# Row-wise softmax: the late loads on ScalarE's DMA queue, and a second and third tile of 5 and 15 rows

## The chip, the core and the metric

The kernel runs on one core of a Trainium2 chip. The metric is the time of one execution on the device, in microseconds (us). Two times occur below: the time of an execution, and its span in the profile, from the first to the last thing that the profile shows.

## What is computed

A softmax with temperature 2 over the last axis of an array of 16 x 1024 x 512 floats, 33.55 MB in and as much out:

```python
x_scaled = x / 2.0
x_max = np.max(x_scaled, axis=-1, keepdims=True)
exp_x = np.exp(x_scaled - x_max)
return exp_x / np.sum(exp_x, axis=-1, keepdims=True)
```

The kernel first computes exp(x / 2) / sum(exp(x / 2)) without the maximum. At the end it counts the rows whose sum lies between 1 and 1e30; if any does not, a second pass with the maximum is run over everything. With the data of this case the second pass is skipped.

## The kernel before

The 16384 rows are spread over 128 partitions, 128 rows of 512 floats in each. "A row" below is one such row in every partition: 128 x 512 floats, 262,144 bytes. The 128 rows are cut into ten tiles (`TILES`, line 10: rows, and place in the on-chip buffer `arena`). `arena` has 98 rows, too few for all 128, so the last two tiles reuse places: tile 8 lies where tiles 0, 1 and 2 were, tile 9 where the end of tile 2 and the start of tile 3 were. `LATE` (line 14) names whose stores must have landed before each may be loaded. These two are called the late loads.

*Loads.* Tile 0 is loaded from SyncE's DMA queue, tiles 1 to 7 from ScalarE's, all issued at the start (`early`, line 146, and `loads`, line 150). A load is one DMA of 128 pieces, one a partition, each as long as the tile's rows. Tile 1 (`SPREAD`) is loaded in three DMAs: all rows but the last over 128 partitions, then the last row over 126 and over 2 partitions (line 111).

*Exponentials.* ScalarE takes the rows in order, in chunks (`HEAD`, then chunks of `E` = 5). For each chunk it waits for `s_go`, which TensorE's queue raises when a tile's load has landed (line 185). It computes the exponential of each row in place, with the row's sum (lines 195 and 269). The chunks of `HEAD`, 23 rows, are straight code; the other 105 rows run in a loop (`exponentials`, line 257).

*Division.* VectorE takes the chunks of a tile in pairs: one reciprocal of the sums (line 160), one multiply in place (line 163). A tile of 15 rows is a pair of 10 rows and a single of 5.

*Stores.* SyncE issues them in order of tiles. `store` (line 127) waits until VectorE is done with the tile. `s_home` counts the landings of stores 0 to 3, on which the late loads depend; `s_end` counts the others, and SyncE waits for it last (line 255). The two late loads stand in SyncE's program among the stores:

```python
for t in (0, 1, 2, 3):
    store(nc.sync, t)
for t, then in ((8, (4,)), (9, (5, 6, 7, 8, 9))):
    nc.sync.wait_ge(s_home[t], landings(LATE[t]))
    load(nc.sync, t)
    for u in then:
        store(nc.sync, u)
```

An engine's program runs in order, so a wait in it holds all that stands behind it. DMAs issued from one engine go into one queue (q1 is SyncE's, q10 ScalarE's in the profile); both queues are served by the same 16 DMA engines. After the exponentials ScalarE's program has only the read of the flag that decides on the second pass.

Of the kernel before, what the change touches and what calls it, by code (L numbers as in the profile page):

```python
# [7 lines left out]


TILES = [  # L10
    (3, 0), (7, 3), (13, 10), (15, 23), (15, 38), (15, 53), (15, 68), (15, 83), (15, 0), (15, 15),
]

LATE = {8: (0, 1, 2), 9: (3,)}
ARENA = 98

HEAD = [3, 4, 3, 5, 4, 4]
E = 5

SPREAD = 1  # L20

LO, HI = 1.0, 1.0e30
G = 8
# [3 lines left out]
def kernel(  # L27
# [5 lines left out]
    nc = tc.nc  # L33
# [10 lines left out]
    n_rows = N // P  # L44
# [13 lines left out]
    tiles, base = [], 0  # L58
# [5 lines left out]
    def dram(ap, t):  # L64
        b, r, _ = tiles[t]
        return ap[b * P : (b + r) * P].rearrange("(p r) d -> p r d", r=r)

    def sb(t):
        _, r, at = tiles[t]
        return arena[:, at : at + r, :]  # L70

    straight = sum(HEAD)
    sizes = HEAD + [E] * ((n_rows - straight) // E)
    starts = [sum(sizes[:k]) for k in range(len(sizes))]
# [14 lines left out]
    s_home = {t: nc.alloc_semaphore(f"s_home{t}") for t in LATE}  # L89
# [17 lines left out]
    def load(eng, t):  # L107
        r = tiles[t][1]
        parts = [(0, P, 0, r)]
        if t == SPREAD:  # L110
            parts = [(0, P, 0, r - 1), (0, 126, r - 1, r), (126, P, r - 1, r)]
        for p, q, lo, hi in parts:
            eng.dma_start(
                out=sb(t)[p:q, lo:hi], in_=dram(xf, t)[p:q, lo:hi]
            ).then_inc(ld[t], 16)
# [6 lines left out]
    def landings(ts):  # L122
        return 16 * len(list(ts))
# [3 lines left out]
    def store(eng, t):  # L127
        eng.wait_ge(s_mul, upto[t])
        eng.dma_start(out=dram(of, t), in_=sb(t)).then_inc(stored_by.get(t, s_end), 16)

    def take(eng, sem, n):
        eng.wait_ge(sem, n).then_inc(sem, -n)  # L132

    def rounds(eng, body, step=1):

        last = n_rows // G
        i = eng.alloc_register("tile")
        eng.wait_ge(s_flag, 1)  # L140
        eng.reg_load(i, flag[0:1, 0:1])
        with eng.While(lambda: eng.snap(i, min_val=0, max_val=last) < last):
            body(eng.snap(i, min_val=0, max_val=last - 1))
            eng.reg_add(i, i, step)
# [9 lines left out]
    def program():  # L154

        nc.vector.memset(ones[:, :], 1.0).then_inc(s_ones, 1)  # L156
        for j, ks in enumerate(pairs):
            b, c = starts[ks[0]], sum(sizes[k] for k in ks)
            a = b % ARENA
            nc.vector.reciprocal(  # L160
                out=recip[:, b : b + c], in_=stats[:, b : b + c]
            )._wait_ge(s_exp, ks[-1] + 1).then_inc(s_rec, 1)
            nc.vector.tensor_mul(  # L163
                out=arena[:, a : a + c],
                in0=arena[:, a : a + c],
                in1=recip[:, b : b + c].unsqueeze(2).to_broadcast([P, c, D]),
            )._wait_ge(s_rec, j + 1).then_inc(s_mul, 1)
        nc.vector.tensor_scalar(  # L168
            out=inside[:, :], in0=stats[:, :], scalar1=LO, scalar2=HI,
            op0=Alu.max, op1=Alu.min,  # L170
        ).then_inc(s_cnt, 1)
        nc.vector.tensor_tensor(  # L172
            out=inside[:, :], in0=inside[:, :], in1=stats[:, :], op=Alu.is_equal
        )._wait_ge(s_cnt, 1).then_inc(s_cnt, 1)
        nc.vector.reduce_sum(  # L175
            out=count[:, :], in_=inside[:, :], axis=mybir.AxisListType.X
        )._wait_ge(s_cnt, 2).then_inc(s_cnt, 1)
        nc.vector.tensor_scalar(  # L178
            out=flag[:, :], in0=total[:, :], scalar1=float(N), scalar2=float(n_rows // G),
            op0=Alu.is_ge, op1=Alu.mult,  # L180
        )._wait_ge(s_tot, 1).then_inc(s_flag, 1)


        for t in range(len(tiles)):
            nc.tensor.wait_ge(ld[t], 48 if t == SPREAD else 16).then_inc(s_go, owner.count(t))
        nc.tensor.wait_ge(s_ones, 1)
        nc.tensor.matmul(  # L187
            total[:, :], lhsT=count[:, :], rhs=ones[:, :], start=True, stop=True
        )._wait_ge(s_cnt, 3).then_inc(s_tot, 1)

        nc.scalar.preload_act_table(Exp)  # L191
        for k, c in enumerate(HEAD):
            take(nc.scalar, s_go, 1)
            for b in range(starts[k], starts[k] + c):
                ins = nc.scalar.activation(  # L195
                    out=arena[:, b], in_=arena[:, b], func=Exp, scale=0.5,
                    accum_out=stats[:, b : b + 1],
                )
            ins.then_inc(s_exp, 1)
        exponentials(straight, n_rows)  # L200

        for t in (0, 1, 2, 3):
            store(nc.sync, t)
        for t, then in ((8, (4,)), (9, (5, 6, 7, 8, 9))):
            nc.sync.wait_ge(s_home[t], landings(LATE[t]))
            load(nc.sync, t)
            for u in then:
                store(nc.sync, u)  # L210

        x_g = xf.rearrange("(t p r) d -> t p r d", p=P, r=G)
        o_g = of.rearrange("(t p r) d -> t p r d", p=P, r=G)
        data = arena[:, 0:G]

        def vector(i):
            take(nc.vector, g_go, 1)
            nc.vector.reduce_max(  # L220
                out=g_max[:, :], in_=data, axis=mybir.AxisListType.X, negate=True
            ).then_inc(g_rec, 1)
            take(nc.vector, g_rec, 1)
            nc.vector.tensor_scalar_mul(
                out=g_max[:, :], in0=g_max[:, :], scalar1=0.5
            ).then_inc(g_neg, 1)
            take(nc.vector, g_exp, 1)
            nc.vector.reciprocal(out=g_sum[:, :], in_=g_sum[:, :]).then_inc(g_rec, 1)
            take(nc.vector, g_rec, 1)
            nc.vector.tensor_mul(  # L230
                out=data, in0=data, in1=g_sum[:, :].unsqueeze(2).to_broadcast([P, G, D])
            ).then_inc(g_mul, 1)

        def scalar(i):
            take(nc.scalar, g_neg, 1)
            for r in range(G):
                ins = nc.scalar.activation(
                    out=arena[:, r], in_=arena[:, r], func=Exp, scale=0.5,
                    bias=g_max[:, r : r + 1], accum_out=g_sum[:, r : r + 1],
                )  # L240
            ins.then_inc(g_exp, 1)

        def gpsimd(_):
            nc.gpsimd.wait_ge(s_end, at_end)
            for i in range(n_rows // G):
                nc.gpsimd.dma_start(out=data, in_=x_g[i]).then_inc(g_ld, 16)
                nc.gpsimd.wait_ge(g_ld, 16 * (i + 1)).then_inc(g_go, 1)
                take(nc.gpsimd, g_mul, 1)
                nc.gpsimd.dma_start(out=o_g[i], in_=data).then_inc(g_st, 16)
                nc.gpsimd.wait_ge(g_st, 16 * (i + 1))  # L250

        rounds(nc.vector, vector)
        rounds(nc.scalar, scalar)
        rounds(nc.gpsimd, gpsimd, n_rows // G)
        nc.sync.wait_ge(s_end, at_end)

    def exponentials(first, end):
        row = nc.scalar.alloc_register(f"row{first}")
        nc.scalar.reg_mov(row, first)
        with nc.scalar.While(lambda: nc.scalar.snap(row, min_val=first, max_val=end) < end):  # L260
            now = nc.scalar.snap(row, min_val=first, max_val=end - E)
            take(nc.scalar, s_go, 1)
            at = nc.s_assert_within(
                now % ARENA, 0, ARENA - E,
                skip_runtime_bounds_check_because="no chunk reaches over the arena's end",
            )
            for r in range(E):
                data = arena[:, r : ARENA - E + 1 + r][:, bass.ds(at, 1)]
                ins = nc.scalar.activation(  # L269
                    out=data, in_=data, func=Exp, scale=0.5,  # L270
                    accum_out=stats[:, r : n_rows - E + 1 + r][:, bass.ds(now, 1)],
                )
            ins.then_inc(s_exp, 1)
            nc.scalar.reg_add(row, row, E)
# [12 lines left out]
    nc.switch_body(here, parent=None, valid_engines=[i.engine for i in jumps])  # L287
    loads()
    program()


# [28 lines left out]
```

## Time and profile before

| what | value |
|---|---|
| time, median of 9 runs | 160.46 us (160.21 to 160.72) |
| the profiled execution | 160.48 us |
| its span | 159.1 us |
| busy: VectorE, ScalarE | 74.9 us, 80.5 us |
| one exponential of a row, L269 | 614 ns, 105 times |
| one multiply of 10 rows, of 5 rows, L163 | 5492 ns, 2824 ns |
| late loads issued by SyncE | at 57.30 and 75.57 us |
| last exponential, last multiply end | 125.1 us, 130.9 us |
| last store, from issue to landing | 28.1 us |

In the profile an instruction is named by its engine and line: DVE is VectorE, ACT is ScalarE, PE is TensorE; SPq and ACTq are the programs of SyncE and ScalarE where they issue DMAs or handle semaphores. "Idle before" an instruction is how long its engine stood still, followed by what ended that. The duration of a DMA issue is that of issuing it; where the data lands is told by "us to landing". A DMA share of 1.00 is all 16 DMA engines busy; in a short window it can pass 1, since a packet is counted where it starts.

### The profile page before, as it was taken

Reading aid. Unit: us, or ns where it says so; the run is one execution under the profiler, and the core shown is the slowest. Engines: PE = TensorE matmul, PEld = TensorE weight load, DVE = VectorE, ACT = ScalarE, POOL = GpSimd, SP = SyncE. Lnnn points to the kernel's source line nnn. Section 1 sums busy time; section 2 is a strip of 40 time slices with the busy share of each in tenths; the row PEclk is TensorE's granted clock in tenths of the full one; section 3 lists DMA queues with packets and bytes.
Section 4 is the critical chain, followed back from the end, with each engine's and each line's share of the span. In section 5 each row is a group of like instructions: output and inputs, shape, how many; then the busy total and the mean of one; then the engine's idle time right before and its main releaser. Section 6 shows DMA issues by size and latency. Waiting matters only on the chain. (4 is left out here: it accounts for less than half of the span.)

```text
span 159.1 us, 624 instructions
## 1 busy us (share of the span) xinstructions
PE 0.2 (0%) x2; PEld 0.1 (0%) x2; DVE 74.9 (47%) x41; ACT 80.5 (51%) x257; POOL 0.2 (0%) x4
## 2 busy tenths in 40 slices
PE   0000000000000000000000000000000000000000
PEld 0000000000000000000000000000000000000000
DVE  0044509809923980099104970089898991000000
ACT  0585595598099306970099204999999400000000
POOL 0000000000000000000000000000000000000000
DMA  7999999999999999999999999999999999999995
GB/s 267 444 377 445 446 421 364 424 452 407 448 446 448 421 440 433 433 433 433 433 433 440 425 440 425 440 425 448 409 433 425 440 425 448 427 440 425 448 417 255
DMA packets 3026, 67.13 MB, mean 422 GB/s; under 512 B 336, under 2 KB 336, under 8 KB 720
## 3 DMA queue, kind: packets, MB, share of 16 engines
q1 hardware_dynamic: 1872, 42.21, 62.0%
q10 hardware_dynamic: 1152, 24.90, 37.0%
q14 instruction: 2, 0.02, 0.0%
HBM read 33.55 MB, written 33.55 MB: 422 GB/s over the span
## 5 line engine op out<-in xcount | busy, mean ns | idle before, releaser
L269 ACT ACTIVATE arena<-arena x105 | 64.3, 614 | 34.5 <-ACTq L132 25.6
L163 DVE TENSOR_TENSOR arena<-arena,recip 128x5120 f32<-128x5120 f32 (+5 forms) x18 | 71.1, 3951 | 0.6
L160 DVE RECIPROCAL recip<-stats 128x10 f32<-128x10 f32 (+5 forms) x18 | 3.5, 197 | 53.5 <-ACT arena L269 38.9
L269 ACT ACTIVATION_READ_ACCUMULATOR arena<-arena x105 | 19.6, 186 | 0.0
L195 ACT ACTIVATE arena<-arena 128x512 f32<-128x512 f32 x23 | 14.1, 615 | 4.3 <-ACTq L132 4.2
L191 ACT ACT_TABLE_LOAD x1 | 1.3, 1283 | 5.9 <-issue 5.9
L195 ACT ACTIVATION_READ_ACCUMULATOR arena<-arena 128x1 f32 x23 | 4.3, 186 | 0.0
L156 DVE MEMSET ones<- 128x1 f32 x1 | 0.1, 59 | 2.7 <-PEq L35 2.7
L187 PE MATMUL total<-ones,count 128*1 128x1 f32 x2 | 0.2, 164 | 131.8 <-DVE count L175 131.8
L172 DVE TENSOR_TENSOR inside<-inside,stats 128x128 f32<-128x128 f32 x1 | 0.3, 293 | 0.0
L175 DVE TENSOR_REDUCE count<-inside 128x1 f32<-128x128 f32 x1 | 0.3, 286 | 0.0
L178 DVE TENSOR_SCALAR flag<-total 1x1 int32<-1x1 f32 x1 | 0.1, 148 | 0.3 <-PE total L187 0.3
L168 DVE TENSOR_SCALAR inside<-stats 128x128 f32<-128x128 f32 x1 | 0.2, 220 | 0.0
L187 PEld LDWEIGHTS total<-ones,count 128*1 128x1 f32 x2 | 0.1, 80 | 131.8 <-DVE count L175 131.8
L304 POOL MEMSET const-bfloat16-1.0<- 128x1 bf16 x1 | 0.1, 102 | 0.0
L304 POOL MEMSET const-uint8-127<- 128x1 uint8 x1 | 0.1, 101 | 0.0
L304 POOL MEMSET const-float32-0.0<- 128x1 f32 x1 | 0.1, 98 | 0.2 <-issue 0.2
L304 POOL MEMSET const-float32-1.0<- 128x1 f32 x1 | 0.1, 98 | 0.0
## 6 DMA issues: line engine op xcount, KB each, us to landing
out_dram<-arena SPq DMA_DIRECT2D x7, 3840.0 KB, 30.8
arena<-in_x_dram ACTq DMA_DIRECT2D x5, 3840.0 KB, 56.9
arena<-in_x_dram SPq DMA_DIRECT2D x2, 3840.0 KB, 37.2
arena<-in_x_dram ACTq DMA_DIRECT2D x1, 3328.0 KB, 15.0
out_dram<-arena SPq DMA_DIRECT2D x1, 3328.0 KB, 26.2
out_dram<-arena SPq DMA_DIRECT2D x1, 1792.0 KB, 22.0
arena<-in_x_dram ACTq DMA_DIRECT2D x1, 1536.0 KB
arena<-in_x_dram SPq DMA_DIRECT2D x1, 768.0 KB, 6.3
```

Of the source, the lines that this page charges most:

```text
L156: nc.vector.memset(ones[:, :], 1.0).then_inc(s_ones, 1)
L160: nc.vector.reciprocal(out=recip[:, b : b + c], in_=stats[:, b : b + c])._wait_ge(s_exp, ks[-1] + 1).then_inc(s_rec, 1)
L163: nc.vector.tensor_mul(out=arena[:, a : a + c], in0=arena[:, a : a + c], in1=recip[:, b : b + c].unsqueeze(2).to_broadcast([P, c, D]),)._w ...
L168: nc.vector.tensor_scalar(out=inside[:, :], in0=stats[:, :], scalar1=LO, scalar2=HI, op0=Alu.max, op1=Alu.min,).then_inc(s_cnt, 1)
L172: nc.vector.tensor_tensor(out=inside[:, :], in0=inside[:, :], in1=stats[:, :], op=Alu.is_equal)._wait_ge(s_cnt, 1).then_inc(s_cnt, 1)
L175: nc.vector.reduce_sum(out=count[:, :], in_=inside[:, :], axis=mybir.AxisListType.X)._wait_ge(s_cnt, 2).then_inc(s_cnt, 1)
L178: nc.vector.tensor_scalar(out=flag[:, :], in0=total[:, :], scalar1=float(N), scalar2=float(n_rows // G), op0=Alu.is_ge, op1=Alu.mult,)._wa ...
L187: nc.tensor.matmul(total[:, :], lhsT=count[:, :], rhs=ones[:, :], start=True, stop=True)._wait_ge(s_cnt, 3).then_inc(s_tot, 1)
L191: nc.scalar.preload_act_table(Exp)
L195: ins = nc.scalar.activation(out=arena[:, b], in_=arena[:, b], func=Exp, scale=0.5, accum_out=stats[:, b : b + 1],)
L269: ins = nc.scalar.activation(out=data, in_=data, func=Exp, scale=0.5, accum_out=stats[:, r : n_rows - E + 1 + r][:, bass.ds(now, 1)],)
L304: nc = _bacc.Bacc("TRN2", target_bir_lowering=False, num_devices=1)
```

## The change

The second and third tile hold 5 and 15 rows instead of 7 and 13. All tiles but the first are now whole chunks of 5 rows, so `HEAD` is one chunk of 3 rows, and the rest runs in two loops of `exponentials`: up to row 83, the end of tile 6, and from there on. Between the two loops, ScalarE waits for the stores that each late load depends on, and issues both late loads. SyncE issues the stores of tiles 0 to 9 and nothing between them.

```diff
 TILES = [
-    (3, 0), (7, 3), (13, 10), (15, 23), (15, 38), (15, 53), (15, 68), (15, 83), (15, 0), (15, 15),
+    (3, 0), (5, 3), (15, 8), (15, 23), (15, 38), (15, 53), (15, 68), (15, 83), (15, 0), (15, 15),
 ]
 
 LATE = {8: (0, 1, 2), 9: (3,)}
 ARENA = 98
 
-HEAD = [3, 4, 3, 5, 4, 4]
+HEAD = [3]
 E = 5
 
 SPREAD = 1
+
+TURN = 83
...
             ins.then_inc(s_exp, 1)
-        exponentials(straight, n_rows)
-
-
-
-        for t in (0, 1, 2, 3):
+        exponentials(straight, TURN)
+        for t, us in LATE.items():
+            nc.scalar.wait_ge(s_home[t], landings(us))
+            load(nc.scalar, t)
+        exponentials(TURN, n_rows)
+
+        for t in range(len(tiles)):
             store(nc.sync, t)
-        for t, then in ((8, (4,)), (9, (5, 6, 7, 8, 9))):
-            nc.sync.wait_ge(s_home[t], landings(LATE[t]))
-            load(nc.sync, t)
-            for u in then:
-                store(nc.sync, u)
```

## The prediction

> **What bounds the kernel now.** I read the page's slices and queues first, then SyncE's own waits, then the timeline around one tile, then windows of the DMA. The page:
>
> ```profile
> span 159.1 us, 624 instructions
> PE 0.2 (0%) x2; PEld 0.1 (0%) x2; DVE 74.9 (47%) x41; ACT 80.5 (51%) x257; POOL 0.2 (0%) x4
> DMA  7999999999999999999999999999999999999995
> GB/s 267 444 377 445 446 421 364 424 452 407 448 446 448 421 440 433 433 433 433 433 433 440 425 440 425 440 425 448 409 433 425 440 425 448 427 440 425 448 417 255
> HBM read 33.55 MB, written 33.55 MB: 422 GB/s over the span
> ```
>
> The reader is to see that the DMA engines are full in every slice but the first and the last, while no compute engine passes 51%. The bytes are fixed, 67.1 MB; at some 433 GB/s they take 155 us, so all but 4 us of the span is transfer. The change can lose by opening a hole in this row. It can win only out of those 4 us.
>
> Next, SyncE's own waits:
>
> ```profile
> SPq L129 <- DVE arena L163: 96.0, 10, 17.9
> SPq L113 <- DMA out_dram<-arena: 28.5, 2, 16.3
> SPq L255 <- DMA out_dram<-arena: 27.7, 1, 27.7
> ```
>
> The middle row holds the two waits ahead of the late loads (L113), the ones the diff takes from SyncE. The last row is the slack that counts: SyncE has issued the last store and waits 27.7 us for it to land. Writing 3.93 MB at 433 GB/s takes 9.1 us, so for over 17 us that store stands behind older stores. The end of compute is covered by that backlog.
>
> The timeline of one tile (start, us, instruction), its ACT row at the tile's first exponential and its SPq row at the stores from it on:
>
> ```profile
> 61.22 0.63 ACT L269 ACTIVATE arena<-arena  x1 [7.98 <-ACTq L132]
> 79.33 0.63 ACT L269 ACTIVATE arena<-arena  x1 [8.81 <-ACTq L132]
> 97.59 0.63 ACT L269 ACTIVATE arena<-arena  x1 [8.97 <-PEq L185]
> ...
> 94.32 36.96 SPq L129 DMA_DIRECT2D out_dram<-arena  x4
> ...
> 112.58 18.69 SPq L129 DMA_DIRECT2D out_dram<-arena  x3
> ```
>
> ScalarE begins tiles 5, 6 and 7 the moment they land (it idled 8 to 9 us before each), 18.11 and 18.26 us apart. Tile 6 goes from 79.33 to its store at 94.32, tile 7 from 97.59 to 112.58: 14.99 us both times (10 rows of exponentials, a multiply of 5.49, one of 2.82, two reciprocals, handovers). The last SPq row ends with the tenth store, issued about 130.9.
>
> Last, the DMA queues of a stretch with both in use (q10 is ScalarE's, q1 SyncE's), and windows before and after ScalarE's queue runs dry near 96:
>
> ```profile
> DMA packets 529, 14.75 MB, mean 434 GB/s; under 512 B 49, under 2 KB 49, under 8 KB 49
> q1 hardware_dynamic: 272, 7.37, 50.3%
> q10 hardware_dynamic: 257, 7.37, 50.2%
> ...
> 61.00:97.00 36.00, 0.00 (x0) 0.00 (x0) 17.26 (x8) 18.58 (x60) 0.00 (x0) 1.00 1.01 437
> 97.00:131.00 34.00, 0.00 (x0) 0.00 (x0) 25.98 (x13) 27.66 (x90) 0.00 (x0) 1.00 1.00 431
> 131.00:148.00 17.00, 0.19 (x2) 0.09 (x2) 0.78 (x4) 0.00 (x0) 0.00 (x0) 1.00 1.00 432
> ```
>
> From 62 to 96 us the two queues moved 7.37 MB each. So a load that runs beside stores takes twice as long as alone: 18.15 us a tile, the spacing above. One queue alone moves almost as much in total (431 to 432 against 437 GB/s).
>
> **The Trainium skill.** "DMA: Bandwidth & Descriptors", section "Queues, rings and completion order", says each DMA engine takes turns between the queues that have work, packet by packet; the even split agrees. Its section "Issuing engines are not separate DMA queues" says that issuing from several engines only saves the issuer's time; 431 against 437 GB/s agrees to 1.4%. Under "Bandwidth" it puts the ceiling at 435 GB/s; the slices of 433 are at it, so steady state has nothing to give.
>
> **The change part by part.**
>
> *Row split and head.* Tiles 0 to 2 still hold 23 rows. Tile 1's load becomes 4 rows of 2 KB in one piece plus the split row, instead of 6 plus one; tile 2 grows to 15. So 0.52 MB move from 12 KB pieces to 30 KB pieces and 1.05 MB from 12 KB to 8 KB ones. The first 11 us ran at 355 GB/s, startup included. I take 0.1 us of loss, with bounds from -0.3 to +0.3 (1.6 of the 3.9 MB moved there change form, 4.4 us' worth; 7% either way is 0.3). The compute of these tiles changes by a few us: store 1 comes about 3 us earlier (5 rows instead of 7: two exponentials and 1.1 us of multiply less, and the load smaller), store 2 about 2 us later (15 rows, whose path is the 14.99 above). Both lie beside loads queued since 5.9 us, so they cost nothing at the end. VectorE keeps 18 pairs. The rolled loop instead of straight code for 20 rows costs 0.1 to 0.2 us a chunk, on an engine idle 4 us and more before each tile.
>
> *Waits and late loads leave SyncE.* Stores 4 to 9 no longer stand behind loads 8 and 9. Removing 28.5 us of waiting gains nothing directly: both DMA queues had work throughout.
>
> *Waits and late loads come to ScalarE.* They stand after row 83, the end of tile 6: about 79.33 + 9.2 = 88.5 us. By then SyncE's waits on stores 0 to 2 and 3 had already passed (57.30 and 75.57, the late-load issues in its timeline), so I take ScalarE's wait as zero; two issues cost about 1 us (nine took 5.80 at the start), under its 9 us of idle time before tile 7. If a wait did bind, tile 7's exponentials would be behind it; with 8 us to spare from 88.5 to 97.6, I don't expect that.
>
> What decides is when the late loads land. Before, load 8 shared q1 with the stores from 57 us, and load 9 was done at 113.4 (issued 75.57, 37.8 us to landing). After, they queue behind load 7 on q10. By load 7's end both versions have moved equal bytes (store 4 takes load 8's place in q1), so tile 7 still starts at 97.59. Stores 5, 6 and 7 are ready from 76.2, 94.3 and 112.6, so q1 stays filled and the even split goes on:
>
> - tile 8 starts at 97.59 + 18.15 = 115.7, its store is ready at 130.7;
> - tile 9 starts at 97.59 + 36.3 = 133.9;
> - store 9 is issued at 133.9 + 14.99 = 148.9, against 130.9 before: 18 us later.
>
> And when does the backlog run out? Before, store 9 landed at 159.0 (28.1 us after issue). Taking back 9.1 us of data and about 0.5 us of completion (the window 158.00 to 159.10 shows no packet), its data started near 149.4 on the last DMA engine, 148.8 on a typical one. The same bytes precede it after, so the queue empties at 148.8 to 149.4, just when store 9 is issued. A store in an empty queue also pays its first-byte delay, which before hid: the first load, issued at 0.00, shows its first packet at about 1.05 us. So store 9's data runs from 149.9 to 159.0 or 159.2, and landing adds 0.5: 159.6 to 159.8 us. All DMA engines start this store together, which recovers some of their spread.
>
> Sum: first-byte delay bare +1.1, spread recovered -0.4, small pieces +0.1, two-queue stretch longer by 36 us -0.1 (bounds 0 and -0.5, from 437 against 431): about +0.65 us. The profiled execution took 160.48 with a span of 159.05, beside a median of 160.46; so 160.48 + 0.65 = 161.1.
>
> **Rivals.**
>
> *B, covered tail, no change (160.5).* Turns are whole packets: 30 KB at a sixteenth of 433 GB/s, one DMA engine's share, is 1.14 us. If store 0, the first to break into the loads, gets in one packet later relative to tile 2 (now of longer packets), each load is 1.14 us earlier and store 9 is issued at 147.8, in time. For: the moment lies near a packet boundary. Against: the slowest of 16 DMA engines sets a landing, so all must shift.
>
> *C, one turn later (162.2).* The opposite shift: +1.14 us on load 9, all exposed. Against: tile 1's smaller load lets tile 2 start earlier, not later.
>
> *D, faster (159.95).* The two-queue stretch ends near 132 instead of 96; at 437 against 431 GB/s over 36 us it saves 36 x 6/437 = 0.5 us. It decides if load 9 also lands early enough, tile 9 starting by 132.7, for store 9 not to bare its delay. For: the two windows. Against: most of their difference is where packets are counted; single slices in both stretches show 433.
>
> *E, the change doesn't do what it says:* a late store would hold ScalarE at row 83 and delay tile 7 and both loads. Store 3 would have to land 13 us later than before; nothing suggests it, and I fold it into C.
>
> **How the numbers follow.** Main forecast 161.1, chance 0.56, own range 160.8 to 161.7 (first-byte delay 0.7 to 1.6, startup -0.2 to +0.3). B 0.20, C and E 0.07, D 0.17. A measurement here can tell about 0.2%, 0.32 us, from no change: D is faster (0.17), B within (0.20), main and C slower (0.63). The range 160.1 to 162.0 leaves out most of D and the upper part of C.
>
> **What would show it.** Right: tile 7 near 97.6, tiles 8 and 9 some 18 us apart, the tenth store issued near 148.9 and landing in under 11 us instead of 28.1, a dip in the DMA row near 149. Wrong: tile 9 starting well before 133 (sharing favours loads, or a shifted turn), no dip at 149, or a dip near 88 (ScalarE's wait binds). A head that is slower or faster by over 0.3 us would show in tile 7's start or in the first six slices.

## The result, and the profile after

The changed kernel takes 161.60 us (161.49 to 161.66, 10 runs), the kernel before 160.49 (31 runs). The ratio is 1.0067 with a 95% interval of 1.0058 to 1.0076: slower by 1.07 us (0.93 to 1.22). The forecast was 161.1 within 160.1 to 162.0.

The page of the changed kernel:

```profile
span 160.1 us, 666 instructions
PE 0.2 (0%) x2; PEld 0.1 (0%) x2; DVE 74.9 (47%) x41; ACT 80.6 (50%) x257; POOL 0.2 (0%) x4
DMA  6999998999899999999998989898999999999795
GB/s 260 395 484 391 467 434 342 484 399 455 384 484 407 453 407 453 438 422 453 407 476 384 476 384 484 378 476 384 476 391 484 399 461 399 461 422 438 299 432 253
```

The bytes and the busy times are those of before. New is the slice with 299 GB/s, third from the end (148 to 152 us): a hole just ahead of the last store. The wavering of the slices before it is no loss: by the packet records of the trace the 16 DMA engines stand idle 0.03 us on average from 11 to 148.2 us, about as in the kernel before (0.04 from 11 to 157.2), and 1.11 us from 148.2 to 150.

SyncE's own waits in the changed kernel:

```profile
SPq L131 <- DVE arena L165: 143.1, 10, 18.1
SPq L254 <- DMA out_dram<-arena: 10.8, 1, 10.8
```

The row of 28.5 us, the waits ahead of the late loads, is gone. So is the slack: the wait after the last store, 27.7 us before, is now 10.8, little more than the 9.1 us that its bytes take. The reading that the experiments below test: the removed wait was worth nothing, and the lost slack decides.

The timeline of the changed kernel, at the first exponential of tiles 7, 8 and 9, and SyncE's stores:

```profile
97.32 0.63 ACT L268 ACTIVATE arena<-arena  x1 [8.90 <-ACTq L134]
...
115.77 0.63 ACT L268 ACTIVATE arena<-arena  x1 [9.16 <-ACTq L134]
...
133.90 0.63 ACT L268 ACTIVATE arena<-arena  x1 [8.84 <-ACTq L134]
...
10.82 138.41 SPq L131 DMA_DIRECT2D out_dram<-arena  x10
```

Tiles 8 and 9 start 18.45 and 18.13 us after the tile ahead of them: each was loaded beside stores, at half the rate. The row of stores ends at 149.23, so the tenth store, an issue of 0.33 us, began at 148.90. Before, that was about 130.9.

The windows around that moment, changed kernel (the last two figures of a row are the DMA share and the GB/s):

```profile
138.00:148.00 10.00, 0.00 (x0) 0.00 (x0) 7.77 (x4) 5.19 (x18) 0.00 (x0) 1.00 1.03 442
148.00:150.00 2.00, 0.19 (x2) 0.09 (x2) 1.65 (x5) 0.00 (x0) 0.00 (x0) 1.00 0.58 246
```

and the kernel before:

```profile
148.00:150.00 2.00, 0.00 (x0) 0.00 (x0) 0.00 (x0) 0.00 (x0) 0.00 (x0) 1.00 1.04 445
```

246 GB/s over 2 us is 0.49 MB, one packet of 30 KB on each of 16 DMA engines, where a full window holds nearly two. By the packet records, the store ahead ends at 148.65 on a typical DMA engine (148.42 to 149.02 over the 16) and the last store's first packets start at 149.72 to 149.88: on a typical engine 1.1 us in which nothing moves.

### The profile page after: what moved, and what is told of

Its sections match the earlier page's. It is cut to its first block, busy times and chain, and to the rows that moved or that the text cites. A ratio compares the mean times of both kernels' runs of the same rounds, so it can differ in the third digit from the quotient of the medians.

```text
span 160.1 us, 666 instructions
## 1 busy us (share of the span) xinstructions
PE 0.2 (0%) x2; PEld 0.1 (0%) x2; DVE 74.9 (47%) x41; ACT 80.6 (50%) x257; POOL 0.2 (0%) x4
## 5 line engine op out<-in xcount | busy, mean ns | idle before, releaser
L268 ACT ACTIVATE arena<-arena x125 | 76.6, 614 | 57.0 <-ACTq L134 57.0
L165 DVE TENSOR_TENSOR arena<-arena,recip 128x2560 f32<-128x2560 f32 (+2 forms) x18 | 71.1, 3951 | 0.6
L162 DVE RECIPROCAL recip<-stats 128x5 f32<-128x5 f32 (+2 forms) x18 | 3.5, 197 | 71.5 <-ACT arena L268 65.4
L268 ACT ACTIVATION_READ_ACCUMULATOR arena<-arena x125 | 23.3, 186 | 0.0
L197 ACT ACTIVATE arena<-arena 128x512 f32<-128x512 f32 x3 | 1.9, 618 | 0.0
L197 ACT ACTIVATION_READ_ACCUMULATOR arena<-arena 128x1 f32 x3 | 0.6, 186 | 0.0
```

What stands on the lines that cost most here:

```text
L162: nc.vector.reciprocal(out=recip[:, b : b + c], in_=stats[:, b : b + c])._wait_ge(s_exp, ks[-1] + 1).then_inc(s_rec, 1)
L165: nc.vector.tensor_mul(out=arena[:, a : a + c], in0=arena[:, a : a + c], in1=recip[:, b : b + c].unsqueeze(2).to_broadcast([P, c, D]),)._w ...
L197: ins = nc.scalar.activation(out=arena[:, b], in_=arena[:, b], func=Exp, scale=0.5, accum_out=stats[:, b : b + 1],)
L268: ins = nc.scalar.activation(out=data, in_=data, func=Exp, scale=0.5, accum_out=stats[:, r : n_rows - E + 1 + r][:, bass.ds(now, 1)],)
```

## The experiments

The theory: the loss is the hole, and the hole is there because load 9 lands so late that the last store comes out of an empty queue. Rivals: the new row split costs it; the queue or ScalarE's part costs it whatever the landing; the moment of the late issue costs it. Ratios are to the kernel before, with 95% intervals.

**The row split alone.** The changed kernel, with the late loads back in SyncE's program:

```diff
-        exponentials(straight, TURN)
-        for t, us in LATE.items():
-            nc.scalar.wait_ge(s_home[t], landings(us))
-            load(nc.scalar, t)
-        exponentials(TURN, n_rows)
+        exponentials(straight, n_rows)
...
-        for t in range(len(tiles)):
+        for t in (0, 1, 2, 3):
             store(nc.sync, t)
+        for t, then in ((8, (4,)), (9, (5, 6, 7, 8, 9))):
+            nc.sync.wait_ge(s_home[t], landings(LATE[t]))
+            load(nc.sync, t)
+            for u in then:
+                store(nc.sync, u)
```

> Only the row split of the change (second and third tile of 5 and 15 rows, one rolled loop); the late loads stay on SyncE among the stores. Theory (the last store comes out of an empty queue because load 9 lands late): load 9 lands near 113, the last store is issued near 131 and lands 28 us later, no hole; time as before, 160.5 (160.2 to 160.8). Rival (the small first tiles and the rolled loop cost the time): 161.4 to 161.6.

Measured: 160.34 us, ratio 0.9988 (0.9981 to 0.9996). By itself the split costs nothing; it gains about 0.19 us. The rival is out.

**The queue move alone.** The kernel before (tiles of 3, 7, 13 rows and its straight code) with the late loads on ScalarE after row 83:

```diff
-        exponentials(straight, n_rows)
+        exponentials(straight, TURN)
+        for t, us in LATE.items():
+            nc.scalar.wait_ge(s_home[t], landings(us))
+            load(nc.scalar, t)
+        exponentials(TURN, n_rows)
```

> Only the move of the late loads to ScalarE's queue after row 83; the row split stays 3, 7, 13. Theory: tile 9 starts near 133.9, the last store is issued near 148.9 into an empty queue and lands 11 us later; 161.5 (161.3 to 161.8), nearly all of the change's loss. Rival (row split): 160.5.

Measured: 162.73 us, ratio 1.0125 (1.0102 to 1.0149). The move carries the whole loss, and more than was expected: the six times lie in two groups, 161.49 and 161.67, then 162.71 to 162.92 with spans about 1.1 us longer. The profile is of the run of 161.49:

```profile
133.90 0.63 ACT L270 ACTIVATE arena<-arena  x1 [8.84 <-ACTq L134]
...
11.05 138.16 SPq L131 DMA_DIRECT2D out_dram<-arena  x10
```

It has tile 9 at 133.90 and the last store issued at 148.9, as expected. The same kernel was run twice more, each time with a trace, for the sake of the upper group:

> The kernel with only the queue move again: its six times fell in two groups, 161.5 to 161.7 and 162.7 to 162.9. Theory (turns are whole packets): the groups differ by one packet of 30 KB, 1.14 us; in a run of the upper group tile 9 starts near 135.0 instead of 133.9 and the last store is issued near 150.3, because store 0 broke into the loads one packet earlier; in the lower group 133.9 and 149.2. Rival (the groups come from the last store's own landing, such as one slow DMA engine): tile 9 near 133.9 in both.

> The same kernel once more, to see the other group if the run before fell in one. The same expectations: tile 9 near 135.0 with a time of 162.7 to 162.9, or near 133.9 with 161.5 to 161.7; rival: 133.9 in both.

Measured: 161.93 and 162.01 us, tile 9 starting at 134.18 and 134.19. They fall between the groups, so neither expectation was met. In them load 9 lands 0.28 us later, and the spans are 0.3 us longer (160.36 and 160.37 against 160.07). What the upper group is, one packet's turn or something else, stays open: no trace shows a run of it. So does another point: the changed kernel differs from this one in the row split alone, and its ten times lie at 161.49 to 161.66, all at the level of the lower group. The effects of split and move taken apart, -0.17 and +2.2 us in the medians, don't add up to the +1.1 of both together.

**Closing the hole from the store's side.** The changed kernel, its last store cut in two, each part issued when its multiply is done:

```diff
-        for t in range(len(tiles)):
+        for t in range(len(tiles) - 1):
             store(nc.sync, t)
+        last = len(tiles) - 1
+        for lo, hi, done in ((0, 10, upto[last] - 1), (10, 15, upto[last])):
+            nc.sync.wait_ge(s_mul, done)
+            nc.sync.dma_start(
+                out=dram(of, last)[:, lo:hi], in_=sb(last)[:, lo:hi]
+            ).then_inc(s_end, 16)
```

> The changed kernel with its last store cut in two: 10 rows as soon as their multiply is done, the last 5 when theirs is. Tile 9 still starts near 133.9. Theory: the first part is issued near 146, 3 us before the queue runs empty, the second near 148.9 behind it; the hole at 149 closes and about 1.0 us comes back: 160.5 (160.2 to 160.8). Rival (the late loads cost by their queue, by ScalarE's time or by the stretch with two queues, not by the hole): stays 161.4 to 161.7.

Measured: 160.23 us, ratio 0.9978 (0.9968 to 0.9987). Its timeline and, in the second fence, its windows:

```profile
133.86 0.63 ACT L274 ACTIVATE arena<-arena  x1 [8.83 <-ACTq L134]
...
145.88 3.29 SPq L213 DMA_DIRECT2D out_dram<-arena  x2
```

```profile
138.00:148.00 10.00, 0.00 (x0) 0.00 (x0) 7.81 (x4) 5.15 (x18) 0.00 (x0) 1.00 1.03 442
148.00:150.00 2.00, 0.19 (x2) 0.09 (x2) 1.65 (x5) 0.00 (x0) 0.00 (x0) 1.00 0.89 379
150.00:158.00 8.00, 0.00 (x0) 0.00 (x0) 0.03 (x1) 0.00 (x0) 0.00 (x0) 1.00 0.93 398
```

Tile 9 starts as late as in the changed kernel (133.86 against 133.90), both late loads are where the change put them, and the time is below that of before. The first part goes out at 145.88 into a queue that is not yet empty; the share from 148 to 150 is 0.89 instead of 0.58. By the packet records the DMA engines now stand idle 0.04 us on average from 11 to 157.2 us, so the rest of the dip to 0.89 is where packets are counted. The hole was the loss. The time fell by 1.37 us (161.60 to 160.23), of which the hole is 1.1; the rest was not separated.

**An earlier issue.** The changed kernel with one size changed:

```diff
-TURN = 83
+TURN = 68
```

> The changed kernel with the late loads issued after row 68 instead of 83, at 70 to 76 us instead of 88. Theory: they still stand behind load 7 in ScalarE's queue, so they land when they did and nothing changes: 161.6 (161.4 to 161.8). Rival (the moment of the issue, or ScalarE's time for it beside tile 7, sets the loss): load 9 some us earlier, 160.5 to 161.0.

Measured: 161.56 us, ratio 1.0062 (1.0049 to 1.0075); tile 9 starts at 133.88, though the loads were issued at 66.99 and 74.18 us instead of 85.21 and 85.59. They stand behind load 7 in their queue; between these two moments, both before load 7 ends, the issue makes no difference.

**A later issue.** `TURN = 98`, after tile 7:

> The changed kernel with the late loads issued after row 98 instead of 83: after tile 7, at 97.4 + 9.2 = 106.6 us, when load 7 has long left the queue. Theory (the landing of load 9 sets the last store, one for one): both loads run beside stores from about 107.7, 18.15 us each, tile 9 starts near 146, the last store is issued near 161 and lands 11 us later: span 172, time 173 to 174. Rival (only the hole of one first-byte delay costs, whatever the landing): 161.6 to 162.5.

Measured: 168.48 us, ratio 1.0491 (1.0470 to 1.0513). Its ScalarE timeline:

```profile
103.34 0.34 ACTq L115 DMA_DIRECT2D arena<-in_x_dram  x1
103.71 0.61 ACTq L115 DMA_DIRECT2D arena<-in_x_dram  x1
126.90 0.63 ACT L268 ACTIVATE arena<-arena  x1 [20.35 <-ACTq L134]
140.70 0.63 ACT L268 ACTIVATE arena<-arena  x1 [4.51 <-ACTq L134]
```

The direction holds, the number missed by 5 us. Tile 9 starts at 140.70, not 146: the issue came 3 us before the exponentials it stands behind were done, and the stores ran dry near 135 (by the packet records), which left load 9 alone on the DMA engines. Against the changed kernel tile 9 is 6.80 us later (140.70 against 133.90), and the span is 6.8 us longer (166.9 against 160.1). One for one, as the theory has it, and far more than one first-byte delay. The packet records have these 6.8 us as two longer holes, one before each of the last two stores: 7.9 us of idle time together, where the changed kernel has 1.1.

**One late load each.** Load 8 back on SyncE ahead of store 4, load 9 alone on ScalarE:

```diff
-        for t, us in LATE.items():
-            nc.scalar.wait_ge(s_home[t], landings(us))
-            load(nc.scalar, t)
+        nc.scalar.wait_ge(s_home[9], landings(LATE[9]))
+        load(nc.scalar, 9)
...
         for t in range(len(tiles)):
+            if t == 4:
+                nc.sync.wait_ge(s_home[8], landings(LATE[8]))
+                load(nc.sync, 8)
             store(nc.sync, t)
```

> The changed kernel with load 8 back on SyncE's queue ahead of store 4, and load 9 alone on ScalarE's after row 83. Theory: load 9 follows load 7 directly, tile 9 starts 18 us earlier, near 115.7, the last store is issued near 131 to 134 behind a backlog: 160.3 (160.1 to 160.6). Rival (a late load on ScalarE's queue costs by itself): 161.0 to 161.6.

Measured: 160.20 us, ratio 0.9971 (0.9961 to 0.9981). SyncE's waits in it:

```profile
SPq L256 <- DMA out_dram<-arena: 27.4, 1, 27.4
SPq L115 <- DMA out_dram<-arena: 13.1, 1, 13.1
```

A late load on ScalarE's queue costs nothing by itself. The slack after the last store is back at 27.4 us, and the 13.1 us that SyncE waits ahead of load 8 harm nobody.

**A longer first tile.** The changed kernel with tiles 0 and 1 as one tile of 8 rows, in one DMA:

```diff
-    (3, 0), (5, 3), (15, 8), (15, 23), (15, 38), (15, 53), (15, 68), (15, 83), (15, 0), (15, 15),
+    (8, 0), (15, 8), (15, 23), (15, 38), (15, 53), (15, 68), (15, 83), (15, 0), (15, 15),
...
-LATE = {8: (0, 1, 2), 9: (3,)}
+LATE = {7: (0, 1), 8: (2,)}
...
-SPREAD = 1
+SPREAD = None
```

> The changed kernel with tiles 0 and 1 made one tile of 8 rows, in one DMA without the split row; everything else stays, the late loads on ScalarE after row 83. Store 0 then breaks into the loads near 29 us instead of 15, so the loads run ahead. Theory: tile 9 (now the ninth, tile 8) starts near 125 to 129, the last store is issued 5 us or more before the queue runs empty, the hole closes though both late loads stay where the change put them, and some of the small pieces' loss at the start goes too: 160.0 (159.7 to 160.5). Rival (the loss belongs to the queue the loads are on): 161.3 to 161.7.

Measured: 160.01 us, ratio 0.9963 (0.9951 to 0.9975), the lowest median here, though its interval overlaps those of 0.9971 (load 8 on SyncE) and 0.9978 (last store cut). The last tile's first exponential and SyncE's wait after the last store:

```profile
128.15 0.63 ACT L268 ACTIVATE arena<-arena  x1 [8.82 <-ACTq L134]
SPq L254 <- DMA out_dram<-arena: 15.0, 1, 15.0
```

Both late loads are still on ScalarE's queue; the first store, issued at 25.18 us instead of 10.82, competes with the loads from later on, so the last load is ahead by 5.7 us and the hole is covered. What part of the gain beyond the hole comes from the missing small pieces was not separated.

The same with `SPREAD = 0`, the first tile's last row in two DMAs of its own:

> As the kernel with a first tile of 8 rows, with that tile's last row loaded by a DMA over 126 and one over 2 partitions, as the kernel before does for its second tile. Theory of the last store: no hole, 159.8 to 160.4, within 0.3 of the run without the split; the split row can only change which DMA engine ends last, by up to 0.6 us (the spread of the last packets in the kernel before). Rival: 161.3 to 161.7.

Measured: 160.37 us, ratio 0.9973 (0.9961 to 0.9986). No hole: SyncE waits 25.7 us after the last store. The medians differ by 0.36 us, a little over the 0.3 expected. The difference is not only the split row, since the three DMAs on SyncE also moved the start of tile 0 from 15.45 to 27.46 us.

## Why the prediction was right

- *DMA-bound, nothing to gain from the removed waits, slack after the last store decides:* right. The kernels with 15 us or more of that wait are at or under the time of before; those with 10.8 us are not. With the last store cut the wait is 9.5 us, but for 1.31 MB, which take 3.0 us at 433 GB/s: 6.5 us are slack, where the changed kernel has 1.7.
- *Even split between the queues, tile 9 at 133.9, last store at 148.9:* 133.90 and 148.90. That they agree to the hundredth is luck: tile 7 started at 97.32 and not at 97.59, and tile 8 came 18.45 us later, where 18.15 was taken.
- *ScalarE's wait at row 83 taken as zero, its issues hidden:* right in effect. The issue at "about 88.5" was wrong: it came at 85.21, while the exponentials of tile 6 ran on to 88.4. The run with row 68 shows that this moves nothing.
- *First-byte delay bare, +1.1:* right in sum, 148.65 to 149.79 on a typical DMA engine, but made up otherwise. From issue to first packet it was 0.89 us there (0.82 on the first engine) instead of 1.05; the other 0.25 is that the queue was empty at 148.65, ahead of the issue, where 148.8 to 149.4 was taken. The landing 11.2 us after the issue also missed the sign "under 11".
- *"Spread recovered -0.4":* wrong, it was about zero, and it is the largest error in the sum. Before, the last data packet ended at 158.54, 0.65 us after a typical DMA engine's (157.89); in the changed kernel at 159.59, again 0.65 us after (158.94). The DMA engines did start the last store together, but one ended late. A window of the changed kernel's DMA from 158 to 160 us, then one from 155.7 to 156:

```profile
q1 hardware_dynamic: 17, 0.03, 4.0%
```

```profile
DMA packets 1, 0.01 MB, mean 27 GB/s; under 512 B 0, under 2 KB 0, under 8 KB 0
q14 instruction: 1, 0.01, 6.4%
```

  0.03 MB after 158 us is a single data packet (the other 16 are the semaphores' writes), started at 158.45 when all others had started by 157.88. The packet records show the same DMA engine at work: a packet stretched to 1.44 us ending at 155.79, the fetch of 8 KB of instructions, 0.31 us, and a packet of 1.23 us, where others take 1.14. So this DMA engine ends at 159.59, the others by 159.02. That they are one engine is read from ends that meet starts. All six traces here whose last store begins in an empty queue show the same: a fetch 6.9 us after its issue, and one end 0.55 to 0.6 us after all others. The run with row 68, for one, has the fetch at 155.75 and one end at 159.56 among others by 159.00. In the kernel before such a fetch comes at 137.52, and its engine is not the one that ends last.
- *"Small pieces +0.1":* wrong in sign; the split alone gained 0.19 us (0.06 to 0.30). The account leaves out that 13 rows of tile 2 go from pieces of 26 KB to 30 KB; whether that is the gain was not tested. The rolled loop, put at 0.1 to 0.2 us a chunk, cost next to nothing: tile 7's exponentials start 0.61 us apart across its three chunks.
- *Two-queue stretch, -0.1:* not separated. Cutting the last store and moving load 8 back give 160.23 and 160.20, the split alone 160.34; the 0.1 fits, but the intervals overlap.
- *The sum:* the four terms of the forecast make 0.7, not the 0.65 written. By the two traces the hole is 1.14 us on a typical DMA engine, the queue was empty 0.15 us earlier than the 148.8 taken, and the spread gave nothing: 1.0 us, beside 1.03 between the spans (159.05 and 160.08) and 1.07 (0.93 to 1.22) between the times. So the mechanism holds, and the forecast of 161.1 was 0.5 us too low mainly by the spread. What an execution spends outside its span scatters from 1.4 to 1.7 us in both kernels.
- *Rivals B and C, a shift by a packet's turn:* not seen in the changed kernel, whose ten times lie within 0.17 us. The queue move alone has groups about 1.2 us apart, and the upper one, 162.7 to 162.9, lies even above what C says. A packet's turn of 1.14 us would fit, but was not shown. D (faster) and a binding wait on ScalarE are out.

## What to carry to other kernels

Where the DMA is full from end to end, don't count the waits; look at how long the last store waits for its landing beyond its own bytes, since that slack is what a reordering can use up. Here a load that was queued beside stores landed at half the rate (18.15 us a tile, where the last store alone moved as many bytes in 9.15), and one put behind other loads inherited their end, however early it was issued. If the last store still comes too late, cut it and send the finished part ahead: here that brought 1.37 us.

## What the runs showed of the hardware

- A DMA issue in ScalarE's program didn't wait for the exponentials ahead of it. The changed kernel's ScalarE timeline:

```profile
85.21 0.34 ACTq L115 DMA_DIRECT2D arena<-in_x_dram  x1
85.27 0.61 ACT L268 ACTIVATE arena<-arena  x1
85.59 0.51 ACTq L115 DMA_DIRECT2D arena<-in_x_dram  x1
...
88.23 0.19 ACT L268 ACTIVATION_READ_ACCUMULATOR arena<-arena  x1
```

  It ran 3 us, five exponentials, ahead of the engine's work; in the run with row 98 likewise (issue at 103.34, with tile 7's exponentials from 97.26 on taking some 9.2 us). So the statement ahead of the prediction, that an engine's program runs in order, needs this much put right: an issue behind exponentials need not wait for their end.
- A fetch of 8 KB of instructions ran among the data on one of the DMA engines, and this engine ended the last store about 0.6 us after the others (159.59 against 159.02).
- Where both queues had work, the DMA engines changed between them at every packet: in the kernel before, from 62 to 96 us, 402 of the 480 packets, of 30 KB each, have a single successor whose start meets their end, and for 399 of them it is a packet of the other queue.
- A store issued into an empty queue showed its first packet 0.82 us after the issue began, and landed 11.2 us after it for 3.93 MB.
